# Expert stage of a hybrid step: token rows, sums and activations held in PSUM, up weights' low part made on GpSimd

## Chip, cores and metric

The kernel runs on one core of a Trainium2 chip. The metric is the device time of one execution in microseconds (us), 4134.7 us in the median of three runs of the kernel before. The engines are named as the profile names them: PE (matrix products), DVE (VectorE), ACT (ScalarE), POOL (GpSimd) and SP (the queue that issues most transfers). SBUF and PSUM are the two on-chip memories; POOL and transfers work on SBUF alone in this kernel.

## What is computed

One layer of a language model on 1024 prompt tokens and 64 sample tokens: RMSNorm, a gated linear recurrence, windowed attention, a merge, and then a retrieval of single-neuron experts, to which the change is confined. For every token the retrieval has chosen 128 of 16384 experts (8 heads, 16 each) and their softmax weights. The expert part is

```python
def expert_block(args):
    xc, ic, gc = args                       # tokens, chosen experts, their weights
    act = jax.nn.gelu(jnp.einsum('cd,ced->ce', xc, expert_u[ic])) * gc
    return jnp.einsum('ce,ced->cd', act, expert_v[ic])
y = hres + expert_block(...)                # D = 1024, float32 throughout
```

## The kernel before

The trunk (norms, attention, recurrence, retrieval) works through three blocks of tokens and takes the first 1920 us. Then comes the expert stage, `dense` (line 904). It treats the tokens in two ways at once.

**All experts for 704 tokens.** The first 704 rows pass through every expert, 128 experts at a time, 128 such chunks; a chunk is called an expert here, as in the loop `for e in grp` (line 923). For each, the up weights `un` and the down weights `vn` are loaded (128x1024 each) and split into a rounded part and a rest, so that a float32 product becomes three matmuls (`mm3`, lines 168 to 170). ACT makes the rounded part (`uh`, `vh`, line 148), and the rest (`ul`, `vl`, line 149) is made by DVE for the up weights (line 928) and by POOL for the down weights (line 948). Two halves of 352 tokens give 24 matmuls each into a PSUM tile `sc`; ACT takes the gelu into an SBUF tile `ge` (line 940), DVE multiplies it by the weights `gt` (line 942), ACT rounds it to `ah`, DVE makes the rest `al`. After three experts (a group) 16 chains of 9 matmuls go into PSUM tiles `ou`, and DVE adds each to the sums `dac0`, `dac1` in SBUF (line 962). An expert is 96 matmuls in all.

**Gathered experts for 384 tokens.** `gather_steps` (line 833) fetches, for a tile of 128 tokens, one row of `expert_u` per token with an indirect transfer that POOL issues (line 842), and DVE multiplies it with the token row `xt` and sums it to one number (line 844, "the u phase"). After 128 such rows a gelu, and then 128 rows of `expert_v` are fetched (line 852) and added, times the activation, to `acc` (line 854, "the v phase"). Three tiles give 768 rows; the tile `row` has four buffers. `pump` (line 858) strews these steps among the first 120 experts.

Every engine works its own queue in order. The order on each queue is made when the program is built, by a scheduler that plays the program through a timing model and picks the instruction that it thinks is ready next; a change of operands, buffers or engines can therefore move instructions on all queues. Up to the expert stage the orders are the same before and after the change.

Of the kernel before, what the change touches and what calls it, by code (L numbers as in the profile page):

```python
# [40 lines left out]
# token blocks of the trunk: (first prompt token, one past the last, carries the sample group)  # L41
BLOCKS = [(0, 256, True), (256, 640, False), (640, 1024, False)]
# rows are kept in the order of the blocks, the sample group after the prompt tokens of its block
# [26 lines left out]
class Kern:  # L70
# [16 lines left out]
    def setup(self, c):  # L87
        """what only the trunk needs"""
# [3 lines left out]
        # 0..127; each four times  # L92
# [5 lines left out]
        # per-channel vectors: convolution (4 taps, bias), the gates' biases, lambda  # L98
        self.vt = c.tile([P, KD, 8], F32, name="vt")
        nc.sync.dma_start(self.vt, i["vecs"])  # L100
        # sp2 = 2 * softplus(-lambda);  softplus(y) = max(y, 0) + log1p(exp(-|y|))
# [23 lines left out]
        # half biases of the two gates  # L125
        self.hb = c.tile([P, KD, 2], F32, name="hb")
        nc.vector.tensor_scalar(self.hb, self.vt[:, :, 5:7], 0.5, None, op0=ALU.mult)
        # attention constants
# [8 lines left out]
        # state carried from block to block  # L137
# [7 lines left out]
    def split(self, hi, lo, src, lo_eng=None):  # L145
        """hi = src rounded to float32r, lo = the rest"""
        nc = self.nc
        nc.scalar.copy(hi, src)  # L148
        return (lo_eng or nc.vector).tensor_tensor(lo, src, f32(hi), op=ALU.subtract)  # L149
# [13 lines left out]
    def mm3(self, ps, terms, first=True, last=True):  # L163
        """ps += sum over terms of (lh + ll).T @ (rh + rl) without ll.T @ rl"""
# [7 lines left out]
    def rsqrt(self, y, v, nm):  # L172
        """y = v ** -0.5 (bit guess, then Newton)"""
# [12 lines left out]
    def load_c(self, src, c0):  # L186
        """128 columns of a [1024, C] weight, split, for proj_c"""
# [8 lines left out]
    def load_n(self, src, c0):  # L196
        """256 columns of a [1024, C] weight, split, in two halves of the rows, for proj_n"""
# [11 lines left out]
    def proj_c(self, src, c0, xh, xl, n):  # L209
        """[128 channels from c0, n tokens]"""  # L210
        wh, wl = self.load_c(src, c0)
        ps = self.mm()
        self.mm3(ps[:, 0:n], [(wh[:, k], wl[:, k], xh[:, k, 0:n], xl[:, k, 0:n]) for k in range(KD)])
        return ps[:, 0:n]

    def proj_n(self, w, xh, xl, c0, r):
        """[r tokens, 256 columns] of a weight chunk"""
# [5 lines left out]
    def norm_T(self, src, r, gb, xh, xl, c0, keep=None):  # L223
        """RMSNorm of src [r, D], transposed and split into xh, xl [:, :, c0:c0 + r]"""
# [42 lines left out]
    def trunk(self, bi, x, raw, bg):  # L267
# [7 lines left out]
        # ---- attention  # L275
# [4 lines left out]
        # ---- gate_attn * branch B  # L280
# [13 lines left out]
        # ---- recurrent branch  # L294
# [6 lines left out]
        # ---- gate_lru * branch A  # L301
# [9 lines left out]
        # ---- out projection, residual  # L311
# [19 lines left out]
        # ---- RMSNorm 2  # L331
# [16 lines left out]
        # ---- product-key retrieval  # L348
# [5 lines left out]
    def qkv(self, bi, c, xh, xl, put=None):  # L354
        """256 columns of q, k, v, to put(t) or to tiles of their own"""
# [11 lines left out]
    def attention(self, bi, xh, xl, ah, al, raw, bg):  # L367
# [12 lines left out]
        # projections of q and k, their norms  # L380
# [33 lines left out]
        def scores(t, j, qT):  # L414
            """softmax numerators over sum, [q, 4 heads, keys]"""
# [5 lines left out]
            for par in range(2):  # L421
                # heads of one parity, whose rows lie in the same half of the partitions
# [23 lines left out]
        def weigh(t, j, sb):  # L446
            """weighted sum of the values, into the transposed branch input"""
# [52 lines left out]
    def smp_scores(self, nP, t, qn, kn, vd, kT):  # L500
        """softmax of the sample group, [head and token, keys] per sequence"""
# [44 lines left out]
    def smp_caches(self, t, kn, vd):  # L546
        """caches handed on: the last 128 of old and new"""
# [41 lines left out]
    def lru(self, bi, n, nP, xh, xl, lh, ll, bg):  # L589
# [3 lines left out]
        # block-diagonal gate weights (two blocks of 64 per 128 channels)  # L593
# [15 lines left out]
        def front(k):  # L609
            """convolution input, convolution"""  # L610
# [28 lines left out]
        def gates(k, xc, A, U, Y):  # L639
            m = k % 2  # L640
            # gates, r = (T + 1) / 2, i = (Ti + 1) / 2;  t = tanh(-log_a / 2), q = a
# [12 lines left out]
            # a = 1 - t (1 + a);  sqrt(1 - a^2) = 2 sqrt(t (1 + a)^2 / 4)  # L654
# [63 lines left out]
    def retrieve(self, bi, tiles, n, yh, yl, bg):  # L718
        """the 16 best keys of either side, for every head"""
# [23 lines left out]
    def choose(self, bi):  # L743
        """the 16 best pairs of every head: their experts and weights"""
# [5 lines left out]
        for t, (c0, r) in enumerate(tiles):  # L750
# [40 lines left out]
            # softmax over the chosen (sorted, the first is the maximum)  # L791
# [30 lines left out]
    def slots_T(self, ft, r, n0):  # L822
        """a tile's slots (two key indices, weight), one column per token"""
# [9 lines left out]
    def gather_steps(self, gp):  # L833
        nc, i, o = self.nc, self.i, self.o
        for t in range(NA // P):
            xt = gp.tile([P, D], F32, tag="xt", name="xt", bufs=1)
            nc.sync.dma_start(xt, self.xn2n_d[t * P:(t + 1) * P, :])
# [10 lines left out]
            acc = gp.tile([P, D], F32, tag="acc", name="acc", bufs=1)  # L848
            nc.sync.dma_start(acc, self.hres_d[ND + t * P:ND + (t + 1) * P, :])
# [6 lines left out]
            nc.sync.dma_start(o["y"][ND + t * P:ND + (t + 1) * P, :], acc)  # L856
# [6 lines left out]
    def build_g(self, bi):  # L863
        """G[chunk, j, i, token]: the weight of expert 128 i + j for a token"""
        nc, sp = self.nc, self.sp
        p0, p1, smp, nP, n, tiles = self.geom(bi)
        for ch in range(ROW0[bi] // CH, (ROW0[bi] + n) // CH):
# [3 lines left out]
            # key indices; weights in three parts, exactly  # L871
# [25 lines left out]
    def dense_x(self):  # L897
        """the columns that pass through every expert, split: rows 0-511 and 512-1023 of hi, of lo"""
# [194 lines left out]
```

## Time and profile before

| | |
|---|---|
| runs | 4132.49, 4134.7, 4149.5 us |
| span of the profiled execution | 4137.6 us |
| PE busy | 3685.5 us (89%) |
| DVE busy | 3523.9 us (85%) |
| POOL busy | 2281.2 us (55%) |
| ACT busy | 1289.3 us (31%) |
| expert stage | first `sc` matmul at 1920.3 us, the end at 4137.6 us |

The span is the time between the first and the last instruction of one profiled execution. A busy share is a mean over stages with different limits, so the rows below look at the expert stage alone, mostly at its 1900 us from 2100 to 4000, in which gathered rows and experts run side by side. An instruction is counted as busy from the time it is started, also while it stands still for a reason that is not a semaphore.

### The profile page before, as it was taken

What the parts mean: (1) busy time and instruction counts of PE and PEld (TensorE: products, weight loads), DVE (VectorE), ACT (ScalarE), POOL (GpSimd) and SP (SyncE); (2) the same over time, 40 slices, a digit from 0 to 9 for tenths busy, and PEclk for the clock granted to TensorE, in tenths of its full rate; (3) what the DMA queues carried; (4) which work ended last, traced back from release to release, by engine and by line L of the source; (5) the groups of instructions that cost most, each with busy time, mean ns of one, the idle gap of its engine ahead of it and who ended that gap; (6) DMA issues with size and microseconds to landing.
All of it is one profiled execution on the core that took longest, in us unless ns stands there. A gap on an engine that the chain in (4) does not pass through costs nothing.

```text
span 4137.6 us, 60745 instructions
## 1 busy us (share of the span) xinstructions
PE 3685.5 (89%) x22734; PEld 3509.0 (85%) x22734; DVE 3523.9 (85%) x6926; ACT 1289.3 (31%) x2337; POOL 2281.2 (55%) x1432
## 2 busy tenths in 40 slices
PE   7989998688887888888999999999989998999898
PEld 6778878578875777887899999998989998989898
DVE  6365878999899989988989889898989998989894
ACT  4454362533335244332222222222222222222221
POOL 3445546575544755644566666565656565656551
PEclk8989999899998989999999999999999999999999
DMA  4335523234430333553288888888888888888882
GB/s 143 107 102 154 154 64 99 75 114 155 165 120 18 88 119 103 188 178 122 85 289 293 288 296 291 298 294 288 292 288 279 295 291 287 290 290 292 284 279 88
DMA packets 505655, 821.75 MB, mean 199 GB/s; under 512 B 34220, under 2 KB 360812, under 8 KB 502000
## 3 DMA queue, kind: packets, MB, share of 16 engines
q1 hardware_dynamic: 394768, 415.18, 31.1%
q0 software_dynamic: 110592, 402.70, 28.3%
q8 instruction: 178, 2.92, 0.3%
q14 instruction: 117, 0.96, 0.1%
HBM read 753.25 MB, written 66.50 MB: 198 GB/s over the span
## 4 chain that ended last, share of the span: by engine, by line
DVE 33%; PE 26%; issue 15%; DMA 9%; POOL 9%; ACT 2%; POOLq 0%; SPq 0%; DVEq 0%; ACTq 0%
POOL row L842 5%; DMA row<-in_expert_v,iA 3%; PE mm L168 3%; PE mm L169 3%; PE mm L170 3%; PE ou L168 3%; PE ou L169 3%; PE ou L170 3%; DMA row<-in_expert_u,iA 3%; DVE oij L886 2%; DVE ul L149 2%; DVE row L844 2%; DVE acc L854 2%; DVE oij L885 2%; DMA vn<-in_expert_v 2%
## 5 line engine op out<-in xcount | busy, mean ns | idle before, releaser
L149 POOL TENSOR_TENSOR wlo<-wraw,whi 128x1024 fp32r<-128x1024 f32 x252 | 639.0, 2542 | 512.6 <-ACT whi L148 469.7
L168 PE MATMUL ou<-ah,vh 128*128 128x352 f32 x2048 | 666.2, 333 | 67.8 <-ACT ah L148 61.8
L170 PE MATMUL sc<-dx,ul 128*128 128x352 f32 x2048 | 671.7, 328 | 50.1 <-DVE ul L149 50.0
L169 PE MATMUL ou<-al,vh 128*128 128x352 f32 x2048 | 673.6, 330 | 27.0 <-DVE al L149 26.5
L168 PE MATMUL sc<-dx,uh 128*128 128x352 f32 x2048 | 670.1, 327 | 9.0 <-ACT uh L148 9.0
L170 PE MATMUL ou<-ah,vl 128*128 128x352 f32 x2048 | 670.4, 329 | 0.0
L169 PE MATMUL sc<-dx,uh 128*128 128x352 f32 x2048 | 668.7, 327 | 0.0
L852 POOL DMA_INDIRECT row<-in_expert_v,iA x384 | 445.1, 1159 | 380.2 <-DVE acc L854 309.6
L842 POOL DMA_INDIRECT row<-in_expert_u,iA x384 | 440.0, 1146 | 367.9 <-DVE row L844 320.6
L844 DVE SCALAR_TENSOR_TENSOR row<-row,xt 128x1024 f32<-128x1024 f32 x384 | 536.3, 1405 | 65.8 <-DMA row<-in_expert_u,iA 64.1
L854 DVE SCALAR_TENSOR_TENSOR acc<-row,hv,acc 128x1024 f32<-128x1024 f32 x384 | 545.3, 1420 | 47.8 <-DMA row<-in_expert_v,iA 45.4
L168 PEld LDWEIGHTS ou<-ah,vh 128*128 128x128 f32 x2048 | 391.2, 193 | 87.7 <-ACT ah L148 76.5
L170 PEld LDWEIGHTS sc<-dx,ul 128*128 128x128 f32 x2048 | 392.5, 192 | 57.7 <-DVE ul L149 57.7
L169 PEld LDWEIGHTS ou<-al,vh 128*128 128x128 f32 x2048 | 396.1, 194 | 33.5 <-DVE al L149 33.2
L149 POOL TENSOR_TENSOR vl<-vn,vh 128x1024 fp32r<-128x1024 f32 x128 | 333.7, 2614 | 123.3 <-ACT vh L148 90.9
L168 PEld LDWEIGHTS sc<-dx,uh 128*128 128x128 f32 x2048 | 393.2, 192 | 9.2 <-ACT uh L148 9.2
L148 ACT CAST whi<-wraw 128x1024 fp32r<-128x1024 f32 x252 | 263.9, 1049 | 429.7 <-PE mm L169 165.5
L170 PEld LDWEIGHTS ou<-ah,vl 128*128 128x128 f32 x2048 | 395.9, 194 | 0.0
L169 PEld LDWEIGHTS sc<-dx,uh 128*128 128x128 f32 x2048 | 393.1, 192 | 0.0
L962 DVE TENSOR_TENSOR dac<-dac,ou 128x352 f32<-128x352 f32 x672 | 332.9, 513 | 44.7 <-PE ou L170 44.3
L148 ACT CAST ah<-ge 128x352 fp32r<-128x352 f32 x256 | 124.2, 486 | 756.9 <-DVE ge L942 756.7
L884 POOL TENSOR_TENSOR oij<-oij,s 128x512 bf16<-128x512 bf16 x176 | 219.4, 1257 | 183.2 <-DVE oij L883 137.4
(284 smaller groups left out, 8618.4 us busy)
## 6 DMA issues: line engine op xcount, KB each, us to landing
wraw<-in_w_in SPq DMA_DIRECT2D x132, 512.0 KB
un<-in_expert_uT SPq DMA_DIRECT2D x128, 512.0 KB
vn<-in_expert_v SPq DMA_DIRECT2D x128, 512.0 KB
g_d<-sg SPq DMA_DIRECT2D x22, 2048.0 KB
gt<-g_d SPq DMA_DIRECT2D x64, 704.0 KB
wraw<-in_peer_w_query SPq DMA_DIRECT2D x48, 512.0 KB
wraw<-in_w_branch_attn SPq DMA_DIRECT2D x24, 512.0 KB
wraw<-in_w_branch_lru SPq DMA_DIRECT2D x24, 512.0 KB
```

Of the source, the lines that this page charges most:

```text
L148: nc.scalar.copy(hi, src)
L149: return (lo_eng or nc.vector).tensor_tensor(lo, src, f32(hi), op=ALU.subtract)
L168: nc.tensor.matmul(ps, lh, rh, start=first and j == 0, stop=False)
L169: nc.tensor.matmul(ps, lh, rl, start=False, stop=False)
L170: nc.tensor.matmul(ps, ll, rh, start=False, stop=last and j == n - 1)
L842: nc.gpsimd.indirect_dma_start(out=row, out_offset=None, in_=i["expert_u"], in_offset=bass.IndirectOffsetOnAxis(ap=ia[:, s:s + 1], axis=0))
L844: nc.vector.scalar_tensor_tensor(row, row, 1.0, xt, op0=ALU.mult, op1=ALU.mult, accum_out=hv[:, s:s + 1])
L852: nc.gpsimd.indirect_dma_start(out=row, out_offset=None, in_=i["expert_v"], in_offset=bass.IndirectOffsetOnAxis(ap=ia[:, s:s + 1], axis=0))
L854: nc.vector.scalar_tensor_tensor(acc, row, hv[:, s:s + 1], acc, op0=ALU.mult, op1=ALU.add)
L884: nc.gpsimd.tensor_tensor(wl, wh, col(4), op=ALU.mult)
L885: nc.vector.tensor_tensor(wm, wh, col(3), op=ALU.mult)
L962: nc.vector.tensor_tensor(ac[k // 4][:, k % 4, a:b], ac[k // 4][:, k % 4, a:b], ps[:, 0:b - a], op=ALU.add)
```

## The change

In the expert stage three operands that stay while others stream past move from SBUF to PSUM: the token row `xt` and the running sum `acc` of the gathered tokens (one PSUM tile `gx` of two banks, used by both in turn), and the activation, which now stays in its `sc` tile through gelu, weighting and split instead of moving to `ge`. [...] The two banks are taken from `sc` and `ou`, which have three tiles each instead of four. The rest of the up weights, `ul`, is made by POOL instead of DVE.

```diff
-    def gather_steps(self, gp):
+    def gather_steps(self, gp, gps):
...
-            xt = gp.tile([P, D], F32, tag="xt", name="xt", bufs=1)
-            nc.sync.dma_start(xt, self.xn2n_d[t * P:(t + 1) * P, :])
+            st = gp.tile([P, D], F32, tag="st", name="st", bufs=2)
+            nc.sync.dma_start(st, self.xn2n_d[t * P:(t + 1) * P, :])
+            xt = gps.tile([P, D], F32, tag="gx", name="xt", bufs=1)
+            nc.scalar.copy(xt, st)
...
-            acc = gp.tile([P, D], F32, tag="acc", name="acc", bufs=1)
-            nc.sync.dma_start(acc, self.hres_d[ND + t * P:ND + (t + 1) * P, :])
+            st = gp.tile([P, D], F32, tag="st", name="st", bufs=2)
+            nc.sync.dma_start(st, self.hres_d[ND + t * P:ND + (t + 1) * P, :])
+            acc = gps.tile([P, D], F32, tag="gx", name="acc", bufs=1)
+            nc.scalar.copy(acc, st)
...
-            nc.sync.dma_start(o["y"][ND + t * P:ND + (t + 1) * P, :], acc)
+            st = gp.tile([P, D], F32, tag="st", name="st", bufs=2)
+            nc.scalar.copy(st, acc)
+            nc.sync.dma_start(o["y"][ND + t * P:ND + (t + 1) * P, :], st)
...
-            self.steps = self.gather_steps(cx.enter_context(tc.tile_pool(name="gp", bufs=1)))
+            gps = cx.enter_context(tc.tile_pool(name="gps", bufs=1, space=PSUM))
+            self.steps = self.gather_steps(cx.enter_context(tc.tile_pool(name="gp", bufs=1)), gps)
...
-            psc = cx.enter_context(tc.tile_pool(name="dpsc", bufs=4, space=PSUM))
-            pou = cx.enter_context(tc.tile_pool(name="dpou", bufs=4, space=PSUM))
+            psc = cx.enter_context(tc.tile_pool(name="dpsc", bufs=3, space=PSUM))
+            pou = cx.enter_context(tc.tile_pool(name="dpou", bufs=3, space=PSUM))
...
-                    self.split(uh, ul, un)
+                    self.split(uh, ul, un, nc.gpsimd)
...
-                        ge = up.tile([P, H], F32, tag="ge", name="ge", bufs=2)
                         ps = psc.tile([P, 512], F32, tag="sc", name="sc")
...
-                        nc.scalar.activation(ge, ps[:, 0:b - a], AF.Gelu_apprx_tanh)
+                        ge = ps[:, 0:b - a]
+                        nc.scalar.activation(ge, ge, AF.Gelu_apprx_tanh)
```

The scheduler puts the queues together anew for this stage. POOL's queue late in the u phase of the second tile, before; `row` is a gathered row, `vl` the rest of an expert's down weights:

```order
L149 TENSOR_TENSOR vl<-vn,vh 128x1024
L842 DMA row<-in_expert_u,iA 128x1024 x14
L149 TENSOR_TENSOR vl<-vn,vh 128x1024
L842 DMA row<-in_expert_u,iA 128x1024
L149 TENSOR_TENSOR vl<-vn,vh 128x1024
L842 DMA row<-in_expert_u,iA 128x1024 x4
L149 TENSOR_TENSOR vl<-vn,vh 128x1024
L842 DMA row<-in_expert_u,iA 128x1024 x16
L149 TENSOR_TENSOR vl<-vn,vh 128x1024 x2
```

and at the same group of experts after:

```order
L149 TENSOR_TENSOR vl<-vn,vh 128x1024
L845 DMA row<-in_expert_u,iA 128x1024
L149 TENSOR_TENSOR vl<-vn,vh 128x1024
L845 DMA row<-in_expert_u,iA 128x1024 x3
L149 TENSOR_TENSOR ul<-un,uh 128x1024
L149 TENSOR_TENSOR vl<-vn,vh 128x1024
L845 DMA row<-in_expert_u,iA 128x1024 x3
L149 TENSOR_TENSOR ul<-un,uh 128x1024
L845 DMA row<-in_expert_u,iA 128x1024 x11
L149 TENSOR_TENSOR ul<-un,uh 128x1024
L845 DMA row<-in_expert_u,iA 128x1024 x3
L149 TENSOR_TENSOR vl<-vn,vh 128x1024 x2
```

Each group has three `ul` more between the same rows; up to 11 row fetches stand ahead of one of them.

DVE's queue in the v phase of the second tile, before (`ul` and the activations `ge`, `al` between the sums):

```order
L854 SCALAR_TENSOR_TENSOR acc<-row,hv,acc 128x1024
L149 TENSOR_TENSOR ul<-un,uh 128x1024
L854 SCALAR_TENSOR_TENSOR acc<-row,hv,acc 128x1024
L942 TENSOR_TENSOR ge<-ge,gt 128x352
L854 SCALAR_TENSOR_TENSOR acc<-row,hv,acc 128x1024
L942 TENSOR_TENSOR ge<-ge,gt 128x352
L149 TENSOR_TENSOR al<-ge,ah 128x352
L854 SCALAR_TENSOR_TENSOR acc<-row,hv,acc 128x1024
L149 TENSOR_TENSOR al<-ge,ah 128x352
L149 TENSOR_TENSOR ul<-un,uh 128x1024
```

and where that phase begins, after (`hv` holds the activations of the gathered rows, `sc` those of the experts, now in PSUM):

```order
L850 TENSOR_TENSOR hv<-hv,gA 128x128
L859 SCALAR_TENSOR_TENSOR acc<-row,hv,acc 128x1024 x2
L950 TENSOR_TENSOR sc<-sc,gt 128x352
L859 SCALAR_TENSOR_TENSOR acc<-row,hv,acc 128x1024
L149 TENSOR_TENSOR al<-sc,ah 128x352
L859 SCALAR_TENSOR_TENSOR acc<-row,hv,acc 128x1024
L950 TENSOR_TENSOR sc<-sc,gt 128x352
L149 TENSOR_TENSOR al<-sc,ah 128x352
```

`ul` is gone from DVE, and the same products and rests work on `sc` instead of `ge`.

## Rows read from the trace of the kernel before

**Rows 1.** Busy time by stretch; columns: stretch, length, five engines, clock, transfers.
```profile
1920.00:2100.00 180.00, 161.19 (x937) 158.14 (x938) 165.37 (x390) 50.52 (x73) 98.23 (x50) 0.93 0.43 139
2100.00:4000.00 1900.00, 1776.26 (x10648) 1746.58 (x10647) 1701.20 (x2266) 415.45 (x669) 1137.70 (x853) 0.97 0.85 290
```
**Rows 2.** Groups by line, 2100 to 4000: busy us, mean ns | idle before, releaser.
```profile
L170 PE MATMUL sc<-dx,ul 128*128 128x352 f32 x1774 | 582.6, 329 | 50.0 <-DVE ul L149 50.0
...
L168 PE MATMUL ou<-ah,vh 128*128 128x352 f32 x1776 | 576.6, 332 | 57.1 <-ACT ah L148 51.3 <-DVE dac L962 4.7 <-issue 1.1
L854 DVE SCALAR_TENSOR_TENSOR acc<-row,hv,acc 128x1024 f32<-128x1024 f32 x370 | 527.4, 1425 | 45.7 <-DMA row<-in_expert_v,iA 43.3 <-DVE dac L962 0.8
L844 DVE SCALAR_TENSOR_TENSOR row<-row,xt 128x1024 f32<-128x1024 f32 x373 | 521.0, 1405 | 64.3 <-DMA row<-in_expert_u,iA 62.7 <-issue 0.8
L852 POOL DMA_INDIRECT row<-in_expert_v,iA x372 | 428.2, 1151 | 371.5 <-DVE acc L854 302.5 <-DMA row<-in_expert_v,iA 24.1 <-issue 16.4
L842 POOL DMA_INDIRECT row<-in_expert_u,iA x370 | 425.8, 1151 | 352.8 <-DVE row L844 311.4 <-issue 26.0 <-DVE al L149 4.6
...
L149 POOL TENSOR_TENSOR vl<-vn,vh 128x1024 fp32r<-128x1024 f32 x111 | 284.4, 2569 | 37.8 <-ACT vh L148 36.2
L149 DVE TENSOR_TENSOR ul<-un,uh 128x1024 fp32r<-128x1024 f32 x111 | 218.3, 1967 | 52.2 <-ACT uh L148 52.2
L149 DVE TENSOR_TENSOR al<-ge,ah 128x352 fp32r<-128x352 f32 x222 | 129.6, 586 | 20.4 <-ACT ah L148 17.1 <-issue 1.1
L942 DVE TENSOR_TENSOR ge<-ge,gt 128x352 f32<-128x352 f32 x222 | 124.7, 564 | 2.3 <-ACT ge L940 2.3
...
L148 ACT CAST uh<-un 128x1024 fp32r<-128x1024 f32 x111 | 116.2, 1046 | 55.2 <-PE sc L169 49.6 <-DMA un<-in_expert_uT 3.3 <-PE ou L168 2.1
```
**Rows 3.** PE in order of time: start us, duration us (first and last of 20).
```profile
2999.42 0.32 PE L169 MATMUL ou<-al,vh 128*128 128x352 f32 x1
...
3002.44 0.32 PE L168 MATMUL ou<-ah,vh 128*128 128x352 f32 x1
```
**Rows 4.** DVE in order of time.
```profile
3007.32 1.22 DVE L844 SCALAR_TENSOR_TENSOR row<-row,xt 128x1024 f32<-128x1024 f32 x1
...
3008.89 1.22 DVE L844 SCALAR_TENSOR_TENSOR row<-row,xt 128x1024 f32<-128x1024 f32 x1
...
3017.99 5.93 DVE L844 SCALAR_TENSOR_TENSOR row<-row,xt 128x1024 f32<-128x1024 f32 x1 [0.65 <-DMA row<-in_expert_u,iA]
```
**Rows 5.** POOL in order of time.
```profile
3009.65 1.27 POOL L842 DMA_INDIRECT row<-in_expert_u,iA  x1 [0.30 <-issue]
...
3018.14 4.69 POOL L149 TENSOR_TENSOR vl<-vn,vh 128x1024 fp32r<-128x1024 f32 x2
```
**Rows 6.** One line's instructions, 2100 to 4000: duration ns min/median/max.
```profile
L844 DVE SCALAR_TENSOR_TENSOR row<-row,xt x373: 1207/1217/6486, 2098.8 to 3708.8; 128x1024 f32<-128x1024 f32 x187
L852 POOL DMA_INDIRECT row<-in_expert_v,iA x372: 932/939/2550, 2389.4 to 3996.2; - x186
L854 DVE SCALAR_TENSOR_TENSOR acc<-row,hv,acc x370: 1269/1277/6465, 2395.7 to 3997.9; 128x1024 f32<-128x1024 f32 x185
L962 DVE TENSOR_TENSOR dac<-dac,ou x592: 503/512/523, 2121.2 to 3997.5; 128x352 f32<-128x352 f32 x198
L149 POOL TENSOR_TENSOR vl<-vn,vh x111: 2348/2415/3390, 2099.2 to 3997.2; 128x1024 fp32r<-128x1024 f32 x111
L149 DVE TENSOR_TENSOR ul<-un,uh x111: 1206/1219/3945, 2103.8 to 3969.3; 128x1024 fp32r<-128x1024 f32 x111
```
**Rows 7.** Two lines of the trunk: one operand in PSUM (`mm`), none there.
```profile
L291 DVE SCALAR_TENSOR_TENSOR mg<-th,mm x24: 486/540/554, 171.3 to 1441.8; 128x384 f32<-128x384 f32 x16, 128x320 f32<-128x320 f32 x8
L653 DVE SCALAR_TENSOR_TENSOR U<-Ti,xc x24: 484/542/2753, 243.9 to 1599.4; 128x384 f32<-128x384 f32 x16, 128x320 f32<-128x320 f32 x8
```
**Rows 8.** Transfers, 2100 to 4000: rate in 40 equal slices, and sums.
```profile
GB/s 305 280 296 294 313 261 292 289 292 295 276 287 300 311 310 275 285 303 290 264 303 274 289 274 281 311 290 314 265 296 303 282 282 284 299 298 285 274 280 292
DMA packets 219546, 550.71 MB, mean 290 GB/s; under 512 B 16417, under 2 KB 95265, under 8 KB 219415
```

## Prediction

> **What bounds the kernel now.** I read the stretches first. In the 1900 us from 2100 to 4000 PE is busy 93% and DVE 90%, POOL 60%, ACT 22% [rows 1]; PE and DVE are both close to full, so the next thing to read is which of them waits for the other. The groups by line tell it: PE stands 50.0 us for `ul` and 57.1 us mostly for `ah`, and both come out of DVE's queue, `ul` directly and `ah` by way of the weighted activation that DVE makes [rows 2]. DVE is the late one.
>
> How much could PE win? The 1774 third matmuls of `sc`, 16 to an expert, are 110.9 experts, 17.13 us each [rows 1, 2]. Undisturbed, the starts of 20 matmuls lie 3.02 us apart, 0.159 us a step [rows 3], and 96 of them make 15.26 us. So 1.87 us an expert, 207 us in the stretch, are lost; beside the waits named this holds restarts and the clock, whose granted mean is 0.97 there [rows 1]. That is the most a change on the other engines can give.
>
> Why is DVE full? Its sums usually take 1.217 or 1.277 us, but up to 6.5 us [rows 6]. The order of time shows the cause: a sum started at 3017.99 lasts 5.93 us, and POOL makes two rests in 4.69 us from 3018.14 on, inside it [rows 4, 5]. DVE stands still while POOL works, and this counts as busy. It is not every DVE instruction: the 592 additions to `dac`, one operand in SBUF and one in PSUM, never leave 503 to 523 ns, while `ul`, with both in SBUF, reaches 3945 [rows 6]. So two SBUF operands are what POOL locks out, and the change leaves no DVE instruction of this stage with two SBUF tensors.
>
> **The change part by part, 2100 to 4000.**
>
> *Locks that go.* Mean less median: 373 sums of the u phase lose 188 ns each, 70 us; 370 of the v phase 148 ns, 55 us; 111 `ul` 748 ns, 83 us [rows 2, 6]. For `al` and `ge`, 222 each, I take `dac`'s 512 ns of the same size as undisturbed: 74 and 52 ns, 28 us together. Sum 236 us.
>
> *`ul` off DVE.* 111 times the undisturbed 1.219 us, 135 us [rows 6]. DVE falls from 1701 to 1330 us, 12.0 us an expert.
>
> *PSUM instead of SBUF on DVE.* As an input, nothing: a two-tensor instruction of the trunk takes 540 ns with one operand in PSUM and 542 with none [rows 7]. Writing PSUM from DVE is in no row. Below, nothing can be gained that the locks don't already count, as 1.277 us for 1024 columns has no wait in it; above, I allow double, the read and the write of `acc` falling on one bank: 370 times 1.28, 474 us. I take the nearest rows, zero, and keep double as an end.
>
> [...]
>
> *`ul` on POOL.* 111 more at the undisturbed minimum of 2.35 us, 261 us [rows 6]. Against it, the fetches get shorter: one issued at 3009.65 takes 1.27 us beside a sum that runs from 3008.89 to about 3010.1, while the median is 0.94 [rows 4 to 6]; 742 times 1.151 less 0.94 is 157 us, and `vl` from 2569 to 2348 ns gives 25 us [rows 2, 6]. POOL goes from 1138 to 1217 us; with the 0.30 us between fetches [rows 5], 742 times, 13.0 us an expert.
>
> *The row loop.* A fetch waits until DVE has let go of the row four before it. From 3007.32 to 3017.99, with no rest on POOL, five sums begin after one another, 2.13 us a row [rows 4]; 742 rows on 110.9 experts are 6.7, so 14.3 us an expert. A rest of 2.35 us on POOL holds up the fetch that falls due in it, some 1.2 us on average and 1.1 fetches; it delays one buffer of four, so two rests cost 2 x 1.1 x 1.2 / 4 = 0.7 us. With it 15.0 us.
>
> *Transfers.* 550.71 MB are 4.97 MB an expert. The mean is 290 GB/s at 0.85 of the engines' time [rows 1, 8]. The best five slices of 40 average 312 GB/s [rows 8]; at that rate an expert's transfers take 15.9 us. This is the longest of the five, and I take it as the new pace: 17.13 to 15.9 is 1.23 us, 136 us in the stretch.
>
> *New waits.* A fourth fewer `sc` and `ou` tiles, and an `sc` is held until DVE has made `al`, not only through the gelu. PE's first matmul into a fourth half waits for it, and all other chains on PE stand behind; the cover is that three halves in the tiles are 3 x 24 matmuls, 11 us of PE, against a gelu, two DVE instructions and a copy of half a us each. I take nothing, and if DVE stands for a row in between (109 us in all for rows [rows 2]) the cover of the `ou` tiles is 3 x 9 matmuls, 4.3 us. `ul` now stands on POOL behind up to 11 fetches, and PE's third matmul of each triple waits for it, with the rest of PE behind; this is covered while the row loop is shorter than an expert, 15.0 against 15.9. At five hand-overs between `xt` and `acc` the tile `gx` must be free before ACT copies for 1.05 us, the length of its 128x1024 cast [rows 2], with DVE's next sum waiting and the activations behind that: 1 to 4 us each, I take 2, 10 us. Three copies back on ACT, at 22% busy, are hidden.
>
> *Outside the stretch.* From 1920 to 2100 about ten `ul`, 24 us, go to a POOL with 82 us free [rows 1]; after 4000 hardly any rows are left. Nothing for both.
>
> *Sum.* The profiled execution spans 4137.6 us, 2.9 above the median of the runs, and I know of no other time of its own. 4137.6 less 136 plus 10 is 4011.6, in the runs' measure 4009: **4010 us**, own range 3970 to 4060.
>
> **Rivals.**
>
> *PE alone sets the pace.* Transfers may go faster than the slices show, as they are at 0.85 of their time at 290 GB/s, which would be 341 at all of it: 14.6 us an expert. Then the whole 207 us less 10 go: 3940, range 3930 to 3970. Against it: DVE's waits for rows, 109 us, stay.
>
> *The lock stays in the v phase.* `acc` takes its factor from `hv`, a column in SBUF, and no row shows such an instruction with a PSUM tensor beside a rest on POOL. If that column goes the same way as a second tensor, POOL's twice as many rests make 110 us of the 55. Half of the experts then keep about today's pace, and half of 136 less 10 is gained: 4076, range 4055 to 4110.
>
> [...]
>
> *POOL's queue takes the place of DVE's: slower.* If rows keep today's mean pace, 1900 us for 742, 2.56 us each, because transfers and not locks set it, two rests on POOL add the 0.7 us to it: 6.7 x 2.56 + 0.7 = 17.8 us an expert, and PE waits for `ul` behind the fetches. 0.7 x 110.9 plus 10 is 88 us more: 4223. It decides from the point where a row takes over 2.4 us (15.9 / 6.7) with the rests on POOL. Against it: the 2.13 us without a lock. For it: PE and DVE both stand still when DVE stands for a row, and transfers get denser.
>
> *DVE writes PSUM at half speed.* 474 us on the v phases, some 55 experts: 8.6 us each on 12.0, 20.6 against 17.1, 193 us more there; the u half gains 68 less 10: 4270.
>
> **How the numbers follow.** Forecast 0.56, PE alone 0.17, lock in the v phase 0.14, POOL's queue 0.09, half-speed writes 0.04. Half a per cent, 20 us, is about what can be told from no change; the bounds are 4114 and 4155. Faster: the first three less a little of the third's upper end, 0.84. Same: that end and mild forms of the queue, 0.06. Slower: 0.10. For 8 in 10 the range takes the forecast, most of PE alone and the third: 3945 to 4105. The two slower ones lie outside.
>
> **What would show it.** The sums' mean falls to its median, near 1.22 and 1.28 us, with no length over 2 us beside a rest on POOL; the fetches' mean falls to 0.94; `vl` and `ul` lie near 2.35. If the v phase alone keeps long sums, the column is the cause; if all its sums are longer, the write is. The slices then show 300 to 315 GB/s, and an expert takes 15.9 us. PE's waits for `ul` from POOL over 100 us would show the queue. Wrong would be: locks gone from DVE and the pace still 17 us.

## The result, and the profile after

The changed kernel takes **3996.2 us** in the median of 4 runs (3995.1 to 3999.96), the kernel before beside it 4133.6: ratio 0.966, 95% interval 0.964 to 0.969. The forecast was 4010, in a range of 3945 to 4105. The profiled execution spans 3998.0 us against 4137.6, 139.6 less. Gathered rows end earlier now, so the stretch read here is 2100 to 3870. The columns of the first view are those of [rows 1]: stretch, length, busy us of PE, PE's weight loads, DVE, ACT and POOL, then clock, share of the transfer engines' time, GB/s.

```profile
1920.00:2100.00 180.00, 167.34 (x981) 162.24 (x981) 162.66 (x398) 52.78 (x78) 127.49 (x71) 0.96 0.49 169
2100.00:3870.00 1770.00, 1728.56 (x10637) 1712.09 (x10636) 1363.40 (x2145) 414.50 (x674) 1235.31 (x968) 1.00 0.90 312
```

PE is busy 98% of the stretch (93% before), DVE 77% (90%). 1770 third matmuls of `sc`, 16 to an expert, are 110.6 experts: **16.0 us an expert against 17.13**, 125 us on 110.9 experts. Another 7 us come before 2100, where 44 more matmuls fit in; the other 8 are not broken down.

The groups by line of that stretch, as in [rows 2]: busy us, mean ns of one, then the engine's idle time before them and what ended it.

```profile
L168 PE MATMUL ou<-ah,vh 128*128 128x352 f32 x1776 | 574.3, 326 | 32.6 <-ACT ah L148 21.3 <-DVE dac L970 11.1
L170 PE MATMUL sc<-dx,ul 128*128 128x352 f32 x1770 | 571.0, 323 | 0.0
L859 DVE SCALAR_TENSOR_TENSOR acc<-row,hv,acc 128x1024 f32<-128x1024 f32 x382 | 490.5, 1284 | 154.4 <-DMA row<-in_expert_v,iA 148.6 <-DVE dac L970 2.8 <-issue 1.0
L847 DVE SCALAR_TENSOR_TENSOR row<-row,xt 128x1024 f32<-128x1024 f32 x362 | 438.9, 1217 | 161.8 <-DMA row<-in_expert_u,iA 152.5 <-issue 5.9 <-ACT xt L840 1.4
L857 POOL DMA_INDIRECT row<-in_expert_v,iA x384 | 362.2, 943 | 267.8 <-DVE acc L859 192.6 <-issue 33.5 <-DMA row<-in_expert_v,iA 16.5
L149 POOL TENSOR_TENSOR vl<-vn,vh 128x1024 fp32r<-128x1024 f32 x112 | 269.2, 2411 | 3.8 <-ACT vh L148 2.2
L149 POOL TENSOR_TENSOR ul<-un,uh 128x1024 fp32r<-128x1024 f32 x111 | 267.5, 2410 | 13.7 <-ACT uh L148 11.6 <-issue 0.2
L950 DVE TENSOR_TENSOR sc<-sc,gt 128x352 f32<-128x352 f32 x222 | 116.8, 526 | 21.3 <-ACT sc L948 12.5 <-issue 6.6 <-ACT uh L148 1.0
L149 DVE TENSOR_TENSOR al<-sc,ah 128x352 fp32r<-128x352 f32 x222 | 115.5, 520 | 48.7 <-ACT ah L148 37.2 <-issue 5.2 <-ACT vh L148 3.5
L850 DVE TENSOR_TENSOR hv<-hv,gA 128x128 f32<-128x128 f32 x3 | 6.5, 2169 | 0.0
```

Read the means against [rows 2]: the sums fell from 1405 and 1425 ns to 1217 and 1284, `al` from 586 to 520, the weighting from 564 to 526, the fetch from 1151 to 943. PE's 50.0 us for `ul` are 0.0. What grew is DVE's wait for rows, 301 us from 106, while POOL's fetches wait for DVE to let go of a row: DVE is no longer late, the rows are. One line still has two SBUF tensors, `hv` (line 850), a small product that the prediction overlooked: its three instances, of 128 columns each, take 0.29 us with no rest on POOL beside it, 1.27 with one and 4.95 with two, where the kernel before has 0.28 us for each of the three and no rest beside any.

That the sums don't stand any more is seen in the lengths, not in the means alone: min/median/max in ns of one line's instructions, as in [rows 6].

```profile
L859 DVE SCALAR_TENSOR_TENSOR acc<-row,hv,acc x382: 1275/1283/1292, 2358.4 to 3868.7; 128x1024 f32<-128x1024 f32 x191
L847 DVE SCALAR_TENSOR_TENSOR row<-row,xt x362: 1207/1217/1224, 2099.4 to 3570.7; 128x1024 f32<-128x1024 f32 x181
```

The longest sum is 1292 ns, where it was 6465 or more [rows 6]. In the order of time (start us, duration us), two sums on DVE from 3010.85, and POOL's rest inside them, as in [rows 4, 5]:

```profile
3009.22 1.29 DVE L859 SCALAR_TENSOR_TENSOR acc<-row,hv,acc 128x1024 f32<-128x1024 f32 x1 [2.48 <-DMA row<-in_expert_v,iA]
...
3010.85 2.61 DVE L859 SCALAR_TENSOR_TENSOR acc<-row,hv,acc 128x1024 f32<-128x1024 f32 x2
```
```profile
3011.75 2.41 POOL L149 TENSOR_TENSOR vl<-vn,vh 128x1024 fp32r<-128x1024 f32 x1
```

The two sums take 1.3 us each beside a rest that runs from 3011.75 to 3014.16. The rate of transfers in 40 slices of the stretch, and their sum [rows 8]:

```profile
GB/s 322 298 293 298 312 315 306 296 312 321 322 301 330 325 317 322 322 330 311 279 312 285 327 322 289 320 323 306 325 308 322 306 317 323 287 314 318 298 314 327
DMA packets 219879, 551.95 MB, mean 312 GB/s; under 512 B 16448, under 2 KB 95296, under 8 KB 219748
```

The mean is the 312 GB/s that the prediction took as the limit. Whether it is one, the experiments say.

A part of the gain is PE's clock, which the prediction held inside its 207 us without a figure of its own. In the kernel before, behind the sum of [rows 4] that stands from 3017.99 on, PE waits 5.46 us for `ul` until 3026.70. The stretch of that wait and the one behind it, columns as in [rows 1]:

```profile
3020.00:3027.00 7.00, 1.54 (x9) 1.24 (x8) 7.00 (x7) 0.00 (x0) 5.01 (x4) 0.93 0.55 162
3027.00:3032.00 5.00, 5.00 (x18) 5.00 (x18) 3.77 (x8) 0.97 (x2) 3.35 (x3) 0.50 0.90 286
```

After the wait the granted clock is 0.50, and the starts of PE's matmuls lie 0.29 us apart instead of 0.16. From 2100 to 4000 there are 296 steps of about 0.29 us (0.28 to 0.305), 39 us more than at 0.16; in the stretch of after there are 50, 7 us, and its mean granted clock is 1.00 against 0.97. The clock falls to 0.50 25 times before and 4 times after in these stretches, each time within 2.3 us of the end of a PE wait of over 0.5 us. By these figures, an estimate, some 33 of the 125 us came by way of the clock, as PE waits less.

### The profile page after: what moved, and what is told of

Read it like the earlier page. It is cut to its first block, busy times and chain, and to the rows that moved or that the text cites. A ratio compares the mean times of both kernels' runs of the same rounds, so it can differ in the third digit from the quotient of the medians.

```text
span 3998.0 us, 60600 instructions
## 1 busy us (share of the span) xinstructions
PE 3641.4 (91%) x22734; PEld 3477.6 (87%) x22734; DVE 3151.0 (79%) x6798; ACT 1290.8 (32%) x2346; POOL 2407.2 (60%) x1560
## 5 line engine op out<-in xcount | busy, mean ns | idle before, releaser
L169 PE MATMUL ou<-al,vh 128*128 128x352 f32 x2048 | 660.1, 325 | 5.3 <-DVE al L149 5.0
L170 PE MATMUL ou<-ah,vl 128*128 128x352 f32 x2048 | 659.0, 324 | 0.0
L859 DVE SCALAR_TENSOR_TENSOR acc<-row,hv,acc 128x1024 f32<-128x1024 f32 x384 | 493.1, 1284 | 157.3 <-DMA row<-in_expert_v,iA 151.6
L847 DVE SCALAR_TENSOR_TENSOR row<-row,xt 128x1024 f32<-128x1024 f32 x384 | 465.5, 1217 | 174.3 <-DMA row<-in_expert_u,iA 165.0
L857 POOL DMA_INDIRECT row<-in_expert_v,iA x384 | 362.2, 943 | 267.8 <-DVE acc L859 192.6
L845 POOL DMA_INDIRECT row<-in_expert_u,iA x384 | 362.4, 944 | 264.4 <-DVE row L847 187.4
L168 PEld LDWEIGHTS sc<-dx,uh 128*128 128x128 f32 x2048 | 386.9, 189 | 20.0 <-DVE al L149 9.8
L169 PEld LDWEIGHTS sc<-dx,uh 128*128 128x128 f32 x2048 | 387.2, 189 | 0.0
L149 POOL TENSOR_TENSOR vl<-vn,vh 128x1024 fp32r<-128x1024 f32 x128 | 309.0, 2422 | 65.6 <-ACT vh L148 38.5
L149 POOL TENSOR_TENSOR ul<-un,uh 128x1024 fp32r<-128x1024 f32 x128 | 310.7, 2427 | 45.7 <-ACT uh L148 43.6
```

The lines of the kernel that those rows point to most:

```text
L168: nc.tensor.matmul(ps, lh, rh, start=first and j == 0, stop=False)
L169: nc.tensor.matmul(ps, lh, rl, start=False, stop=False)
L170: nc.tensor.matmul(ps, ll, rh, start=False, stop=last and j == n - 1)
L845: nc.gpsimd.indirect_dma_start(out=row, out_offset=None, in_=i["expert_u"], in_offset=bass.IndirectOffsetOnAxis(ap=ia[:, s:s + 1], axis=0))
L847: nc.vector.scalar_tensor_tensor(row, row, 1.0, xt, op0=ALU.mult, op1=ALU.mult, accum_out=hv[:, s:s + 1])
L857: nc.gpsimd.indirect_dma_start(out=row, out_offset=None, in_=i["expert_v"], in_offset=bass.IndirectOffsetOnAxis(ap=ia[:, s:s + 1], axis=0))
```

## The experiments

Two questions: what gave the 137 us, and what sets the 16.0 us. For the first the theory is the **lock** (DVE instructions with two SBUF operands stand while POOL makes a rest); its rival is the **load** (135 us of `ul` taken off a full DVE). For the second the theory of the prediction is **transfers** at 312 GB/s; its rival is the **row loop** with its four buffers.

| kernel | median us | ratio to before, 95% interval | us an expert, 2100 to 3800 | DVE standing there, us |
|---|---|---|---|---|
| before | 4134 to 4145 | 1 | 17.0 | 212 |
| after | 3996.2 | 0.966 (0.964 to 0.969) | 16.0 | 7 |
| after, `ul` back on DVE | 4007.5 | 0.968 (0.966 to 0.969) | 16.1 | 47 |
| before, `ul` on POOL | 4245.7 | 1.026 (1.024 to 1.027) | 17.9 | 417 |
| after, rows and sums in SBUF | 4210.1 | 1.017 (1.015 to 1.019) | 17.8 | 328 |
| after, activations in SBUF | 4154.6 | 1.003 (1.002 to 1.005) | 17.2 | 339 |
| before, `vl` on DVE too | 3990.6 | 0.964 (0.962 to 0.966) | 16.1 | 4 |
| after, six row buffers | 3948.1 | 0.953 (0.949 to 0.956) | 15.5 | 9 |
| after, half of the down weights loaded | 4002.9 | 0.965 (0.961 to 0.969) | 15.9 | – |
| after, half of the gathered rows | 3943.9 | 0.952 (0.948 to 0.955) | 15.5 | – |
| after, rows over 124 experts | 3990.5 | 0.962 (0.959 to 0.966) | 15.9 | – |
| six buffers and 124 experts | 3938.7 | 0.952 (0.950 to 0.953) | 15.6 | – |

An expert is counted as 16 third matmuls of `sc`. "Standing" is a line's mean less its undisturbed length, times its count, over DVE's sums, weightings and rests; the undisturbed lengths are 1217 ns (u phase, `ul`, `vl`), 1277 (v phase) and 512 (`al` and the weighting), nearly as in the prediction. The row of before is the prediction's 236 us, read in this shorter stretch.

### `ul` back on DVE

```diff
-                    self.split(uh, ul, un, nc.gpsimd)
+                    self.split(uh, ul, un)
```

> The changed kernel with the up weights' rest on DVE again; operands stay in PSUM. Lock theory (what cost the time were DVE instructions with two SBUF operands standing while POOL makes a rest): only ul still has two SBUF operands, POOL makes one rest an expert, so DVE gets 135 us of work and up to 83 us of standing back, 14.0 us an expert, below the pace of 16.0; most of the gain stays: 4010 to 4050 us. Load theory (the gain is ul's leaving DVE): most of the gain is lost: 4090 to 4130 us.

Measured: 4007.5 us, ratio 0.968 (0.966 to 0.969), which overlaps that of the change. The one line that can be caught again (2100 to 3800, columns as above), and the stretch:

```profile
L149 DVE TENSOR_TENSOR ul<-un,uh 128x1024 fp32r<-128x1024 f32 x107 | 170.3, 1592 | 16.3 <-ACT uh L148 13.3 <-issue 2.1 <-PE sc L168 0.4
```
```profile
2100.00:3800.00 1700.00, 1654.75 (x10126) 1638.35 (x10125) 1445.68 (x2172) 396.50 (x646) 985.56 (x818) 0.99 0.90 310
```

`ul` stands 1592 less 1217 ns, 107 times, 40 us, and DVE is busy 85%. Nearly the whole gain is there all the same, a little below the lock theory's range, so the load was not what it came from. By the medians the move of `ul` is worth 11 us, and that is not told from none. It isn't the load's price alone either: with `ul` on DVE, POOL has one rest an expert less between its row fetches.

### `ul` on POOL alone

```diff
-                    self.split(uh, ul, un)
+                    self.split(uh, ul, un, nc.gpsimd)
```

> The kernel before with one edit, the up weights' rest on POOL; all operands stay in SBUF. Lock theory: POOL makes two rests an expert and locks out sums, weightings and rests twice as long, 153 us of standing become about 306, ul's 218 us leave: DVE 1636 us in the stretch in place of 1701, with more and longer stands: 4100 to 4170 us. Load theory: 4040 to 4080 us.

Measured: 4245.7 us, ratio 1.026 (1.024 to 1.027): slower, with 135 us of work less on DVE. The groups by line, 2100 to 3800:

```profile
L844 DVE SCALAR_TENSOR_TENSOR row<-row,xt 128x1024 f32<-128x1024 f32 x371 | 572.5, 1554 | 41.4 <-DMA row<-in_expert_u,iA 40.5
L168 PE MATMUL ou<-ah,vh 128*128 128x352 f32 x1511 | 496.5, 338 | 128.2 <-ACT ah L148 121.6 <-DVE dac L962 6.4
L854 DVE SCALAR_TENSOR_TENSOR acc<-row,hv,acc 128x1024 f32<-128x1024 f32 x256 | 394.5, 1541 | 20.4 <-DMA row<-in_expert_v,iA 18.3 <-DVE dac L962 0.8
L149 DVE TENSOR_TENSOR al<-ge,ah 128x352 fp32r<-128x352 f32 x190 | 216.5, 1139 | 44.4 <-ACT ah L148 43.0 <-issue 0.6
L942 DVE TENSOR_TENSOR ge<-ge,gt 128x352 f32<-128x352 f32 x190 | 202.5, 1066 | 22.6 <-ACT ge L940 21.2 <-ACT uh L148 0.8 <-issue 0.3
```

With twice the rests on POOL every DVE line is longer than in [rows 2]; `al` and `ge` nearly double. The standing goes from 212 to 417 us, and PE pays by way of `ah`, 121.6 us. The load theory falls. The lock theory has the direction right, but its range ends 76 us too low: it foresaw 306 us of standing in 1900, and 417 in 1700 came.

### Only the activations in PSUM

```diff
-            st = gp.tile([P, D], F32, tag="st", name="st", bufs=2)
-            nc.sync.dma_start(st, self.xn2n_d[t * P:(t + 1) * P, :])
-            xt = gps.tile([P, D], F32, tag="gx", name="xt", bufs=1)
-            nc.scalar.copy(xt, st)
+            xt = gp.tile([P, D], F32, tag="xt", name="xt", bufs=1)
+            nc.sync.dma_start(xt, self.xn2n_d[t * P:(t + 1) * P, :])
...
-            st = gp.tile([P, D], F32, tag="st", name="st", bufs=2)
-            nc.sync.dma_start(st, self.hres_d[ND + t * P:ND + (t + 1) * P, :])
-            acc = gps.tile([P, D], F32, tag="gx", name="acc", bufs=1)
-            nc.scalar.copy(acc, st)
+            acc = gp.tile([P, D], F32, tag="acc", name="acc", bufs=1)
+            nc.sync.dma_start(acc, self.hres_d[ND + t * P:ND + (t + 1) * P, :])
...
-            st = gp.tile([P, D], F32, tag="st", name="st", bufs=2)
-            nc.scalar.copy(st, acc)
-            nc.sync.dma_start(o["y"][ND + t * P:ND + (t + 1) * P, :], st)
+            nc.sync.dma_start(o["y"][ND + t * P:ND + (t + 1) * P, :], acc)
```

> The changed kernel with token rows and sums in SBUF again (activations in PSUM, three sc and ou tiles, ul on POOL). Lock theory: the sums have two SBUF operands against two rests an expert, 125 us of standing become about 250, their mean length rises to 1.5 to 1.7 us: 4080 to 4150 us. Load theory: 4000 to 4040 us, as ul is off DVE.

Measured: 4210.1 us, ratio 1.017 (1.015 to 1.019), far beyond what was expected. By line, 2100 to 3800:

```profile
L845 DVE SCALAR_TENSOR_TENSOR row<-row,xt 128x1024 f32<-128x1024 f32 x366 | 627.2, 1720 | 87.2 <-DMA row<-in_expert_u,iA 85.9 <-DVE dac L964 0.4
L168 PE MATMUL sc<-dx,uh 128*128 128x352 f32 x1532 | 512.9, 335 | 79.5 <-DVE al L149 79.5
L855 DVE SCALAR_TENSOR_TENSOR acc<-row,hv,acc 128x1024 f32<-128x1024 f32 x277 | 493.7, 1782 | 57.4 <-DMA row<-in_expert_v,iA 54.4 <-issue 1.3 <-DVE dac L964 0.4
```

The sums stand 503 and 505 ns each, 324 us in 1700, where the prediction read 125 in 1900 from before; twice the rests alone would make 250 of that. With `al` and the weighting out of reach, more of the rests meet a sum. PE waits 79.5 us for `al`, which frees the `sc` tile and comes behind the sums in DVE's queue: the wait of which the prediction took that 11 us of PE would cover it, true only while DVE doesn't stand.

### Only rows and sums in PSUM

```diff
-                        ge = ps[:, 0:b - a]
-                        nc.scalar.activation(ge, ge, AF.Gelu_apprx_tanh)
+                        ge = up.tile([P, H], F32, tag="ge", name="ge", bufs=2)
+                        nc.scalar.activation(ge, ps[:, 0:b - a], AF.Gelu_apprx_tanh)
```

> The changed kernel with the activations in SBUF again (rows and sums in PSUM, ul on POOL, three sc and ou tiles). Lock theory: 444 short instructions of DVE stand against two rests an expert, 28 us become about 56, but each stand of up to 2.4 us lies on PE's way to ah: 4010 to 4050 us. Load theory: no difference from the changed kernel, 3990 to 4005 us.

Measured: 4154.6 us, ratio 1.003 (1.002 to 1.005); expected was most of the gain, and none is there. By line, 2100 to 3800:

```profile
L168 PE MATMUL ou<-ah,vh 128*128 128x352 f32 x1577 | 525.1, 335 | 97.7 <-ACT ah L148 92.4 <-DVE dac L970 4.6 <-issue 0.4
L847 DVE SCALAR_TENSOR_TENSOR row<-row,xt 128x1024 f32<-128x1024 f32 x372 | 448.4, 1214 | 44.8 <-DMA row<-in_expert_u,iA 40.8 <-issue 2.3 <-ACT xt L840 0.6
L950 DVE TENSOR_TENSOR ge<-ge,gt 128x352 f32<-128x352 f32 x198 | 321.4, 1623 | 16.6 <-ACT ge L948 13.6 <-issue 2.5
L149 DVE TENSOR_TENSOR al<-ge,ah 128x352 fp32r<-128x352 f32 x198 | 219.2, 1107 | 37.8 <-ACT ah L148 30.6 <-issue 2.2 <-ACT vh L148 2.1
```

The row sums are free (1214 ns). But the weighting now takes 1623 ns and `al` 1107, where both took under 600 in [rows 2]: 338 us of standing on instructions that lost 25 before in the same 1700 us. In the order of time, DVE and then POOL:

```profile
3001.07 3.08 DVE L149 TENSOR_TENSOR al<-ge,ah 128x352 fp32r<-128x352 f32 x1 [0.55 <-ACT ah L148]
```
```profile
3001.34 2.40 POOL L149 TENSOR_TENSOR ul<-un,uh 128x1024 fp32r<-128x1024 f32 x1
```

`al`, half a us of work, stands through the whole of POOL's `ul`. What is no longer caught at one instruction is caught at the next one with two SBUF operands that DVE comes to, and these two lie on the way to `ah`, for which PE waits 92.4 us. So the parts of the change don't add up: either alone, with two rests on POOL, gains nothing or loses; together they leave the rests next to nothing to catch. These two runs separate the lock best: but for a few copies on ACT they have the work of the changed kernel on every engine, the same two rests on POOL among them, and differ from it in where operands of DVE lie; they are 214 and 158 us slower.

### No rests on POOL at all

```diff
-                    vsub = self.split(vh, vl, vn, nc.gpsimd)
+                    vsub = self.split(vh, vl, vn)
```

on the kernel before: every operand stays in SBUF, and DVE makes both rests.

> The kernel before with one edit: the rest of the down weights on DVE too, so that POOL makes no rest in the expert stage; all operands in SBUF. It tells whether POOL's reading is what makes DVE stand. Lock theory: every DVE instruction with two SBUF operands falls to its undisturbed length (1.22, 1.28, 0.51 us), 236 us of standing go, 135 us of work come: DVE 1600 us in place of 1701 in the stretch, 4040 to 4100 us. Rival (the stands come from DVE's own operands or from transfers): lengths as before, DVE 1840 us: 4200 us or more.

Measured: 3990.6 us, ratio 0.964 (0.962 to 0.966), not told from the change. By line and by stretch, 2100 to 3800:

```profile
L844 DVE SCALAR_TENSOR_TENSOR row<-row,xt 128x1024 f32<-128x1024 f32 x372 | 452.1, 1219 | 95.4 <-DMA row<-in_expert_u,iA 94.4
L854 DVE SCALAR_TENSOR_TENSOR acc<-row,hv,acc 128x1024 f32<-128x1024 f32 x343 | 438.5, 1279 | 46.0 <-DMA row<-in_expert_v,iA 44.5
L149 DVE TENSOR_TENSOR ul<-un,uh 128x1024 fp32r<-128x1024 f32 x106 | 129.0, 1217 | 12.2 <-ACT uh L148 12.2
L942 DVE TENSOR_TENSOR ge<-ge,gt 128x352 f32<-128x352 f32 x212 | 108.7, 517 | 5.7 <-DMA gt<-g_d 5.7
```
```profile
2100.00:3800.00 1700.00, 1657.81 (x10207) 1640.93 (x10206) 1527.32 (x2297) 399.00 (x636) 841.64 (x715) 0.99 0.91 311
```

Every two-SBUF instruction in these rows has its undisturbed length, although nothing went to PSUM; DVE does 126 us of `vl` more than before and is busy 90%, and the kernel is as fast as the change, 49 us below the range that the lock theory gave it. So the other party of the lock is POOL's rest, and DVE's own operands and the transfers don't make the stands. The time is less clean than the lengths: with its rests POOL also loses what stood between its row fetches, and that is a second thing that this run takes away. The loop over the row buffers shows it, from one fetch to the fetch four rows later. After the change a lap takes 9.5 us in the mean: 6.8 from the fetch to the start of its sum, 1.25 for the sum, 1.5 from there to the next fetch. Here it is 9.5 as well, but 7.8, 1.25 and 0.4. What POOL's rests cost there, the way from the fetch to its sum costs here. So that a DVE at 90% is as fast as one at 77% doesn't show that the load is free.

### What sets the new pace: six row buffers

```diff
-                row = gp.tile([P, D], F32, tag="row", name="row", bufs=4)
+                row = gp.tile([P, D], F32, tag="row", name="row", bufs=6)
```

in both phases; to make room, `st` and `hv` have one buffer instead of two.

> The changed kernel with six row buffers in place of four (paid for by one st and one hv buffer less). What sets the pace of 16.0 us an expert now, against 15.3 of PE alone? Transfer theory (312 GB/s is what the transfers give): DVE's waits for rows get fewer but the pace stays, 3985 to 4000 us. Loop theory (a fetch waits for the row four before it): six buffers take the loop from 15.0 to 10 us an expert and the pace to 15.4: 3925 to 3960 us.

Measured: 3948.1 us, ratio 0.953 (0.949 to 0.956). The stretch, two groups and the rate in 40 slices, 2100 to 3800:

```profile
2100.00:3800.00 1700.00, 1693.96 (x10522) 1691.83 (x10521) 1352.51 (x2132) 413.16 (x667) 1225.41 (x962) 1.00 0.91 323
```
```profile
L168 PE MATMUL ou<-ah,vh 128*128 128x352 f32 x1755 | 563.8, 324 | 5.5 <-ACT ah L148 2.5 <-DVE dac L970 2.5 <-issue 0.4
L859 DVE SCALAR_TENSOR_TENSOR acc<-row,hv,acc 128x1024 f32<-128x1024 f32 x382 | 490.9, 1285 | 70.3 <-DMA row<-in_expert_v,iA 63.3 <-issue 5.2 <-ACT acc L854 0.4
```
```profile
GB/s 350 336 325 353 327 306 364 331 308 352 350 310 314 337 325 350 340 316 339 353 320 314 329 314 304 298 327 294 346 293 304 315 313 294 301 331 327 318 300 315
```

PE is busy 99.6%, its idle time before the first `ou` matmul falls from 32.6 us (21.3 of it for `ah`) to 5.5 (2.5), an expert takes 15.5 us. The slices reach 364 GB/s, and their mean is 323, so 312 was what the rows asked for, not what the transfers could give. The row loop holds, the transfers fall.

### Fewer bytes: half of the down weights

```diff
-                    vn = up.tile([P, D], F32, tag="raw", name="vn", bufs=3)
-                    nc.sync.dma_start(vn, i["expert_v"][e * P:(e + 1) * P, :])
+                    if e % 2 == 0:
+                        vn = up.tile([P, D], F32, tag="raw", name="vn", bufs=3)
+                        nc.sync.dma_start(vn, i["expert_v"][e * P:(e + 1) * P, :])
```

> The changed kernel without every second load of down weights (an odd expert takes the tile of the even one before it, so 64 of 128 chunks of down weights are left out of the result); all engines have the same work, transfers 5% fewer bytes (4.97 to 4.71 MB an expert). Transfer theory: at 312 GB/s 15.1 us an expert, so PE's 15.3 to 15.5 bounds: 3935 to 3965 us. Loop theory: 3980 to 4000 us.

Measured: 4002.9 us, ratio 0.965 (0.961 to 0.969), not told from the change, and just above the loop theory's range.

```profile
2100.00:3800.00 1700.00, 1660.33 (x10237) 1641.58 (x10236) 1313.99 (x2088) 399.82 (x653) 1196.16 (x937) 1.00 0.87 297
```

An expert moves 297 GB/s by 15.9 us, 4.7 MB instead of 5.0; under a limit of 312 GB/s it would take 15.1 us. It takes 15.9: the rate fell, and the time stayed. Transfers don't set the pace.

### Fewer rows: every second one

```diff
-            for s in range(NSLOT):
+            for s in range(0, NSLOT, 2):
...
-            ngat = 2 * NSLOT * (NA // P)
+            ngat = NSLOT * (NA // P)
```

in both phases, with `hv` cleared first.

> The changed kernel with every second gathered row only (half of the chosen experts of 384 tokens are left out), 3.3 rows an expert: transfers 3.2 MB, loop 7.5 us, DVE 8 us an expert. Both theories: PE alone bounds, 15.3 to 15.5 us an expert: 3915 to 3950 us. If it stays above 3970, something else holds PE: the clock, or the activations' way through ACT and DVE.

Measured: 3943.9 us, ratio 0.952 (0.948 to 0.955).

```profile
2100.00:3800.00 1700.00, 1692.72 (x10542) 1688.44 (x10542) 933.54 (x1569) 417.63 (x671) 869.92 (x582) 1.00 0.60 207
```

With DVE at 55%, POOL at 51% and 207 GB/s, an expert still takes 15.5 us: this is PE's own floor in this stage. Six row buffers with all the rows reach it too.

### Rows over 124 experts, and both together

```diff
-PACE = 120
+PACE = 124
```

> The changed kernel with the gathered rows strewn among 124 experts in place of 120. Transfer and loop theories alike: 3% fewer rows an expert in the stretch, pace 15.6 to 15.9, and four experts fewer at PE's own pace behind: 3980 to 3996 us. If the last rows come so late that the sums wait for them, 4000 us or more.

Measured: 3990.5 us, ratio 0.962 (0.959 to 0.966), not told from the change. The edit did less than it says: from 2100 to 3800 there are 704 row sums on 106.8 experts, 6.60 an expert, where the change has 6.70. One and a half per cent of the rows can't separate anything here; the run is inconclusive.

With the six buffers:

> Six row buffers and the rows strewn among 124 experts. PE alone bounds with six buffers already (3948 us against 3944 with half the rows), so no difference: 3940 to 3950 us; if the last sums come too late, 3950 to 3965 us.

Measured: 3938.7 us, ratio 0.952 (0.950 to 0.953), the lowest median of all, just under the expected range, and not told from six buffers alone.

```profile
2100.00:3800.00 1700.00, 1694.99 (x10554) 1693.58 (x10553) 1331.30 (x2108) 412.45 (x665) 1202.87 (x940) 1.00 0.88 317
```

PE is full (99.7%); what is left of this stretch is matmuls.

## Why the prediction was right, and where not

**Locks that go: right.** Forecast 236 us of standing gone; sums, `al` and weighting are within 14 ns of the undisturbed lengths. That the lock was the cause of the time is shown by the two halves of the change: with the same work on every engine and the same rests on POOL, putting either set of operands back into SBUF brings 328 or 339 us of standing and takes the whole gain away. The runs that move a rest point the same way, but each changes POOL's row queue too: without rests on POOL the gain is there, and with twice the rests and nothing in PSUM the kernel is 2.6% slower.

**`ul` off DVE: right as a count, no gain seen.** DVE's busy time an expert is 12.3 us against the 12.0 forecast. With DVE at 85% (`ul` back) or 90% (`vl` too) the pace is 16.1 us, but POOL then makes one or two rests fewer, so the load's own price stays open.

**PSUM instead of SBUF: right.** Writing `acc` to PSUM costs 7 ns (1284 against 1277), `sc` in and out 14 ns (526 against 512). The half-speed write, the far end of the range, is refuted by the 1284 ns.

**`ul` on POOL: right.** 2.41 us a rest (2.35 forecast), 0.943 us a fetch (0.94), POOL busy 11.2 us an expert (11.0 forecast, 13.0 with the time between fetches), and PE waits 0.0 us for `ul`. The rival of POOL's queue, slower than before, is refuted; but rests that hold up fetches, its mechanism, are what the next but one point turns on.

**The rival of the column: refuted.** All 382 sums of the v phase, with their factor from an SBUF column, lie between 1275 and 1292 ns.

**The row loop: mis-sized, and this is the one that mattered.** The prediction had 14.3 us an expert plus 0.7 for the rests on POOL, 15.0, under the transfers' 15.9. Measured in the trace of after, from one fetch to the fetch four rows later: 8.23 us in the mean of 251 laps without a rest on POOL in them, 10.22 in 469 with one (8.63 and 12.43 before). At 6.7 rows an expert the first is 8.23 / 4 x 6.7 = 13.8 us, below the 14.3; but 469 of 720 laps are 2.0 us longer, 2.0 x 0.65 / 4 x 6.7 = 2.2 us, not 0.7. Together 16.0, the measured pace. That this sum meets the pace proves nothing, as a mean lap, divided by four buffers and taken 6.7 times, is the time of an expert whatever sets it. That the loop does set it is shown by the two buffers more, and the laps show where the time goes. Of the 2.0 us, 1.8 lie between the end of a sum and the next fetch into its buffer (2.10 against 0.30): buffers that stand empty until POOL is done. Of these 2.1 us, POOL makes rests in 1.15 and issues other fetches in 0.55. Summed over laps, 469 times 2.0 on some 215 rests is 4.4 us a rest, where the prediction had 1.1 fetches of 1.2 us, 1.3: it counted the fetch that falls due in a rest, and not those that queue behind it or behind the next rest.

**Transfers as the new pace: wrong in cause, right in size.** The step "this is the longest of the five, and I take it as the new pace" failed: 5% fewer bytes changed nothing, and two more row buffers moved the same bytes faster, up to 364 GB/s. That 15.9 was met is luck: the row loop, which stood at 15.0 in the prediction, takes 16.0. A mean rate of before, even of its best slices, showed what was asked for.

**PE alone: its floor was 15.5 us, not 15.26.** The 0.159 us a step of [rows 3] held for 20 matmuls; over whole experts it is 15.5 / 96 = 0.162. With the waits of an expert gone, 17.13 to 15.5 on some 120 experts is 196 us, and six buffers take 185 to 197 (4133.6 or 4145.4 less 3948.1). So the rival "PE alone", which the prediction put at 3940, is not refuted as a place to get to: two row buffers were missing.

**Hand-overs: smaller.** DVE waits 1.4 us for `xt`; 10 us were put in.

**Outside the stretch: nothing forecast, 15 us there.** The forecast's 136 less 10 in the stretch meet the 125 measured; the 7 us before 2100 and the 8 that are not broken down were not foreseen.

So of the 137 us measured the forecast had 124. Its cause, the lock, is right; that its size came so close is in part luck, as a wrong ceiling lies close to the real one.

## What to carry to other kernels

Where a DVE instruction has a maximum far above its median (here 6486 ns against 1217 and 6465 against 1277), and an engine next to it is inside a two-operand instruction at that time, count the standing as a wait, and look at which operands both have; then either take all such DVE instructions of the stage out of reach or take the other engine's work away, since here, with half of them mended, the standing on the rest grew to 324 us (sums) or 338 (`al` and the weighting), from 212 on all of them before, also on those that PE waits for. The rate of 312 GB/s read here was what was asked for, as 323 were moved with six row buffers; before such a rate is used as a ceiling, a run with fewer bytes or more buffers has to say so. In the loop over four row buffers a rest on POOL delayed the fetch that fell due in it and those queued behind, 4.4 us of laps a rest where the prediction had 1.3.

## What the runs showed of the hardware

- DVE's instructions with two SBUF tensors stood beside POOL's rests, which have two as well (up to 6.5 us in the kernel before); the sums with an SBUF and a PSUM tensor didn't after the change, also with an SBUF column as a third operand: 1275 to 1292 ns in all 382. A start that the profile shows as earlier was not enough: with only rows and sums in PSUM, `al`, started 0.27 us before POOL's `ul`, stood until 0.41 us after its end (3001.07 to 3004.15 beside 3001.34 to 3003.74). In the kernel before, from 2100 to 4000, 66 DVE instructions of 1024 columns with two SBUF tensors were running when a rest began that was the first to meet them. Of the 26 that had started up to 0.65 us before the rest 25 stood; all 40 that had started 0.74 us or more before it took 1.21 to 1.29 us, and there the rest was the longer one, 2.65 us in the mean against 2.41 undisturbed. So here either engine was at times the one that stood.
- The fetches that POOL issues were held up too: with two-SBUF sums on DVE the indirect fetch takes 1143 and 1214 ns in the mean in the two phases (before, with `vl` on DVE too and no rests on POOL), after the change, with one operand in PSUM, 943 and never over 969.
- The standing was not tied to an instruction's share of time. 25 us on `al` and the weighting (2100 to 3800) became 338 when the sums were taken out of reach and a second rest was added.
- After a wait of 5.46 us PE's granted clock was 0.50 for the next 5 us (3027 to 3032 in the kernel before).
